# Output weights two tiles ahead, eight low parts of h on GpSimd, and the attention norm's factors inside the first weights

## The chip, the cores and the metric

One core of a Trainium2 chip. The metric is the device time of one execution in microseconds (us), and of several runs the median. Engines are named as in the profile: PE (TensorE, matrix products), ACT (ScalarE), DVE (VectorE), POOL (GpSimd), and SP, whose queue issues most of the loads and stores. Each engine executes its own instructions in the order in which they stand in the program, and waits on semaphores where it needs another's result.

## The reference

One decoder layer with model width 1024, 1024 tokens, eight sliding-window heads and eight forgetting-attention heads, and an MLP of width 4096, in float32:

```python
xn = rmsnorm(x, attn_norm_g)
proj = jnp.einsum('bsd,de->bse', xn, w_in)
...
out_a = swa_sinks_attention(qa, ka, va, sink_logits)
...
out_b = forgetting_attention(qb, kb, vb, log_f)
mixed = jnp.concatenate([out_a.reshape(b, s, A_Q_W), out_b.reshape(b, s, B_W)], axis=-1)
x = x + jnp.einsum('bse,ed->bsd', mixed, w_out)
hn = rmsnorm(x, mlp_norm_g)
hid = jnp.square(jax.nn.relu(jnp.einsum('bsd,df->bsf', hn, w_up)))
x = x + jnp.einsum('bsf,fd->bsd', hid, w_down)
```

## The kernel before

**Products.** Every operand of a product is split into a rounded high part (type fp32r) and a low part, the rest. A product is three passes: high by high, high by low, low by high. `split` (line 75) makes the two parts of one tile: a cast on one engine, and a subtraction, which reads the raw tile and the high part, on another. Both inputs of the subtraction are in SBUF.

**Start.** NWARM = 8 products on zeros come first on PE. Then the first projection runs over eight steps k of the contraction (lines 193 to 223). For each k, SP loads 128 rows of x transposed (`xr`, in two halves of 512 tokens) and 128 x 384 weights (`wr`); DVE casts the weights, POOL makes their low part (DVE for k = 0), and ACT and DVE make the two parts of x times the norm's factor `ga`. `ga` is eight columns of the small tile `vt`, which ACT's queue loads at the very start. The eight sums `qps0` to `qps7` are 128 tokens each. At k = 0 all high-by-high products come first; from k = 1 on the three passes of a token block stand together.

**Attention** fills the time up to about 437 us; other projections and the first halves of the output products (`out_first`, which leaves eight partial sums in the DRAM tensor `part_d`) are laid between its heads. The last products of output tiles 0 and 4 come at its end.

**Output stage, 437 to 477 us.** The output has eight tiles `dt` of 128 model columns by 1024 tokens. The order is 0, 4 (ahead), then 1, 5, 2, 6, 3, 7. For each, `out_weights` loads four 128 x 128 weight blocks (`wor`) and splits them into `wos` (cast on ACT, low part on POOL), `out_products` makes 24 products of 512 columns into two PSUM banks `po0`, `po1`, and `out_finish` ends the tile:

- SP loads the partial sum from `part_d` into `h`; DVE adds the two banks (line 958, one input in PSUM); SP stores `h` to `h_d`. Tiles 0 to 3 share one slot for `h`, tiles 4 to 6 another, so the next load into a slot waits for the store.
- `h` is split at once for the up products, which follow a seven-product scheme (Strassen's, in Winograd's form) over halves of the model width and of the tokens: seven operands `bh1` to `bh7` (high) and `bl1` to `bl7` (low). `bh1` comes from tiles 0 to 3, `bh2` and `bh3` from 4 to 7, and the others from sums `ts` of a tile dt and its partner dt + 4: DVE makes the sums (lines 965 and 977), ACT casts them, and DVE makes the low parts (`sum_splits`, line 985). Such a pair is one t of four.

The up weights follow from the middle of this stage: `wur` is the raw load, `wus` are four sums of its blocks made by DVE, and `wu` is a split operand (cast on ACT; low part on DVE for products 2, 6 and 5, on POOL for the others). Up products stand in the order `UP = (1, 2, 3, 6, 7, 5, 4)` and go to banks `pu1` to `pu7`, k running over t. A split operand's slot (w0 to w6) is shared with `h`, `xt` and `wos`, so a cast into it waits for what stood there.

**What sets the order.** The kernel's calls are placed by a scheduler, which has its own estimate of each instruction's length and moves instructions of an engine past each other. `tc.issue_after` keeps an instruction behind another one. From 477 us on the up products and then the down products (`pd`) run to the end, PE without a gap.

Of the kernel before, what the change touches and what calls it, by code (L numbers as in the profile page):

```python
# [16 lines left out]
P = 128  # L17
D = 1024
# [12 lines left out]
NWARM = 8  # L31
# [24 lines left out]
def hybrid_layer(  # L56
# [18 lines left out]
    def split(hi, lo, src, hi_eng, lo_eng):  # L75
        if hi_eng is nc.scalar:
            hi_eng.copy(hi, src)  # L77
        else:
            hi_eng.tensor_copy(hi, src)
        lo_eng.tensor_tensor(out=lo, in0=src, in1=hi.bitcast(F32), op=ALU.subtract)  # L80

    def rsqrt(pool, out, t, shape, tag):
# [26 lines left out]
    nc.scalar.dma_start(vt[:, :36], vecs)  # L109
    ga, gm, vec, bfb, snk = (  # L110
        vt[:, a:b] for a, b in ((0, 8), (8, 16), (16, 20), (20, 28), (28, 36))
    )
    nsnk = cp.tile([P, NH], F32, name="nsnk")
    nc.vector.tensor_scalar_mul(nsnk, snk, -1.0)
    gqk = cp.tile([P, 2], F32, name="gqk")
    for i in range(2):
        nc.vector.tensor_tensor(
            out=gqk[:, i : i + 1], in0=vec[:, 2 * i : 2 * i + 1],
            in1=vec[:, 2 * i + 1 : 2 * i + 2], op=ALU.mult,
        )  # L120

    nc.vector.tensor_scalar_mul(gqk, gqk, -0.25 / math.sqrt(HD))
# [53 lines left out]
    def w_tiles(n):  # L176


        w = wp.tile([P, 2 * WL], F32R, tag="w", name="w", bufs=8)
        wr = wp.tile([P, WN], F32, tag="wr", name="wr", bufs=3)  # L180
        lo = 384 if n == 384 else 400
        return wr[:, :n], w[:, :n], w[:, lo : lo + n]
# [10 lines left out]
    for k in range(KT):  # L193
        xr = ap2.tile([P, S], F32, tag="s", name="xr", bufs=NS)
        wr, wh, wl = w_tiles(384)
        if k == 0:
            nc.sync.dma_start(wr, w_a0[:, k, :])
            nc.scalar.preload_act_table_set("natural_log_exp_and_others")
        nc.sync.dma_start(xr[:, halves[0]], xT[k * P : (k + 1) * P, halves[0]])
        if k:  # L200
            nc.sync.dma_start(wr, w_a0[:, k, :])
        nc.sync.dma_start(xr[:, halves[1]], xT[k * P : (k + 1) * P, halves[1]])
        split(wh, wl, wr, nc.vector, nc.gpsimd if k else nc.vector)
        for cs in halves:
            hi, lo = (x_part(j, k, cs) for j in range(2))
            nc.scalar.activation(hi, xr[:, cs], AF.Copy, scale=ga[:, k : k + 1])
            last_x = nc.vector.scalar_tensor_tensor(  # L207
                out=lo, in0=xr[:, cs], scalar=ga[:, k : k + 1],
                in1=hi.bitcast(F32), op0=ALU.mult, op1=ALU.subtract,
            )  # L210
        passes = ((0, wh), (0, wl), (1, wh))
# [21 lines left out]
    def load_w(src, n):  # L233
        his, los = [], []
        for k in range(KT):
            wr, wh, wl = w_tiles(n)
            nc.sync.dma_start(wr, src[:, k, :])
            with tc.high_priority(offset=HPO):
                split(wh, wl, wr, nc.scalar, nc.gpsimd)
            his.append(wh)  # L240
            los.append(wl)
        return his, los
# [609 lines left out]
    nout = [0]  # L852

    def out_weights(dt, e0):
# [3 lines left out]
        w = slot(f"w{i % 2}", "wos", [2, 4, P], F32R)  # L858
        split(w[:, 0], w[:, 1], wr, nc.scalar, nc.gpsimd)
# [83 lines left out]
    part = {}  # L943
# [345 lines left out]
def _layout(x, attn_norm_g, w_in, b_forget, q_norm_a, k_norm_a, sink_logits,  # L1289
# [16 lines left out]
            [cols(attn_norm_g), cols(mlp_norm_g), two(q_norm_a), two(k_norm_a),  # L1306
             two(q_norm_b), two(k_norm_b), rep(b_forget), rep(sink_logits)], axis=1
        ),
        "w_a0": rows(np.concatenate([qa[:, :P], w_in[:, 512:768]], axis=1)),
# [34 lines left out]
```

## Time and profile before

| | us |
|---|---|
| runs of the kernel before | 1095.04, 1093.57, 1093.83 (median 1093.83) |
| the profiled execution | 1092.15 |
| its span, first to last instruction | 1090.4 |
| start to the first real product | 5.4 |
| projections and attention | 5.4 to 437 |
| output stage | 437 to 477 |
| up products | 477 to 782 |
| down products and the end | 782 to 1090.4 |
| ACT busy | 569.9 |
| POOL busy | 362.5 |

Times in the profile are from the span's start. A row of a timeline has the start, the length, the engine, the kernel's line, the operation and its tiles (out <- in), and how many followed without a gap (x); in brackets stands how long the engine had been idle before, and what ended that. A matmul's length is longer than its distance to the next one, because they overlap.

### The profile page before, as it was taken

Reading aid. Unit: us, or ns where it says so; the run is one execution under the profiler, and the core shown is the slowest. Engines: PE = TensorE matmul, PEld = TensorE weight load, DVE = VectorE, ACT = ScalarE, POOL = GpSimd, SP = SyncE. Lnnn points to the kernel's source line nnn. Section 1 sums busy time; section 2 is a strip of 40 time slices with the busy share of each in tenths; the row PEclk is TensorE's granted clock in tenths of the full one; section 3 lists DMA queues with packets and bytes.
Section 4 is the critical chain, followed back from the end, with each engine's and each line's share of the span. In section 5 each row is a group of like instructions: output and inputs, shape, how many; then the busy total and the mean of one; then the engine's idle time right before and its main releaser. Section 6 shows DMA issues by size and latency. Waiting matters only on the chain.

```text
span 1090.4 us, 15689 instructions
## 1 busy us (share of the span) xinstructions
PE 1078.7 (99%) x5557; PEld 933.5 (86%) x5557; DVE 777.7 (71%) x1327; ACT 569.9 (52%) x1013; POOL 362.5 (33%) x352
## 2 busy tenths in 40 slices
PE   9999999999999999999999999999999999999998
PEld 8999999999997888778888888888888888888886
DVE  7377677767765676998686869867675876674395
ACT  5558588666766756554545444353633433333331
POOL 5672523435434634333222232322222222231100
PEclk9999999999999999999999999999999999999999
DMA  9401212335656565663545543443998886665523
GB/s 308 141 27 48 72 37 61 115 87 154 209 192 221 167 223 174 212 231 126 198 179 179 189 153 135 149 170 145 333 390 311 299 289 227 241 228 181 174 87 116
DMA packets 96079, 195.69 MB, mean 179 GB/s; under 512 B 7376, under 2 KB 19584, under 8 KB 96000
## 3 DMA queue, kind: packets, MB, share of 16 engines
q1 hardware_dynamic: 95856, 194.66, 51.4%
q8 instruction: 44, 0.72, 0.3%
q14 instruction: 35, 0.29, 0.1%
q10 hardware_dynamic: 144, 0.02, 0.0%
HBM read 141.61 MB, written 53.04 MB: 179 GB/s over the span
## 4 chain that ended last, share of the span: by engine, by line
PE 82%; DMA 6%; DVE 6%; issue 2%; ACT 2%; POOL 1%; SPq 0%; ACTq 0%; POOLq 0%; DVEq 0%
PE pu L73 28%; PE pd L73 28%; PE ps L73 10%; PE po L73 5%; PE spb L73 3%; PE pvb L73 2%; PE tpb L725 2%; PE sp L73 1%; PE pv L73 1%; DMA wr<-in_w_b_dram 1%; DMA xq<-in_x_dram 1%; PE tpa L554 1%; DMA xr<-in_xT_dram 1%; DMA mixs_d<-mixn 1%; DVE x L207 1%
## 5 line engine op out<-in xcount | busy, mean ns | idle before, releaser
L73 PE MATMUL pd<-hx,wx 128*128 128x512 f32 (+1 forms) x1350 | 304.9, 388 | 0.0
L73 PEld LDWEIGHTS pd<-hx,wx 128*128 128x128 f32 x1350 | 252.7, 188 | 52.2
L73 PE MATMUL pu<-bh,wu 128*128 128x512 f32 x896 | 276.6, 390 | 1.0 <-ACT bh L947 1.0
L73 PE MATMUL ps<-w,x 128*128 128x384 f32 (+1 forms) x960 | 199.0, 345 | 0.4 <-DVE z L451 0.3
L73 PEld LDWEIGHTS pu<-bh,wu 128*128 128x128 f32 x896 | 168.1, 188 | 36.4 <-ACT bh L947 1.4
L73 PE MATMUL pu<-bl,wu 128*128 128x512 f32 x448 | 174.0, 389 | 0.0
L73 PEld LDWEIGHTS ps<-w,x 128*128 128x128 f32 x960 | 165.2, 189 | 3.7 <-DVE z L451 0.6
L77 ACT CAST hx<-hr 128x1024 fp32r<-128x1024 f32 x56 | 59.1, 1055 | 176.2 <-PE pd L73 171.2
L80 POOL TENSOR_TENSOR wx<-wda,wx 128x1024 fp32r<-128x1024 f32 x24 | 64.5, 2687 | 196.4 <-ACT wx L77 196.4
L80 DVE TENSOR_TENSOR hx<-hr,hx 128x1024 fp32r<-128x1024 f32 x56 | 72.2, 1297 | 71.0 <-ACT hx L77 71.0
L73 PEld LDWEIGHTS pu<-bl,wu 128*128 128x128 f32 x448 | 84.1, 188 | 17.7 <-issue 0.2
L73 PE MATMUL po<-mix,wos 128*128 128x512 f32 x384 | 94.8, 396 | 1.0 <-ACT wos L77 1.0
L73 PEld LDWEIGHTS po<-mix,wos 128*128 128x128 f32 x384 | 70.5, 188 | 15.5 <-ACT wos L77 1.5
L80 POOL TENSOR_TENSOR wu<-wus,wu 128x512 fp32r<-128x512 f32 x32 | 45.6, 1426 | 113.0 <-ACT wu L77 113.0
L80 POOL TENSOR_TENSOR wu<-wur,wu 128x512 fp32r<-128x512 f32 x32 | 44.2, 1380 | 102.5 <-ACT wu L77 102.5
L1018 DVE TENSOR_TENSOR ht<-hb 128x512 f32<-128x512 f32 x32 | 21.8, 723 | 62.8 <-ACT hb L1073 62.8
L394 DVE TENSOR_TENSOR ptl<-tpb,pth 128x512 fp32r<-128x512 f32 (+1 forms) x80 | 49.5, 631 | 21.9 <-ACT pth L393 18.9
L80 POOL TENSOR_TENSOR w<-wr,w 128x384 fp32r<-128x384 f32 (+1 forms) x47 | 51.5, 1106 | 40.1 <-ACT w L77 29.4
L77 ACT CAST wu<-wus 128x512 fp32r<-128x512 f32 x64 | 38.0, 618 | 48.3 <-PE pu L73 39.9
L77 ACT CAST wx<-wda 128x1024 fp32r<-128x1024 f32 x56 | 58.5, 1049 | 6.6 <-DMA wda<-in_w_d_dram 6.6
L689 ACT ACTIVATE sb<-sb,nmb 128x128 f32<-128x128 f32 (+3 forms) x64 | 49.8, 779 | 22.7 <-DVE nmb L683 22.6
L1072 ACT ACTIVATE hb<-hb 128x2048 f32<-128x2048 f32 x16 | 30.7, 1917 | 48.0 <-DVE hb L1021 47.9
(210 smaller groups left out, 1839.3 us busy)
## 6 DMA issues: line engine op xcount, KB each, us to landing
wda<-in_w_d_dram SPq DMA_DIRECT2D x34, 1024.0 KB, 9.2
hr<-hid_d SPq DMA_DIRECT2D x56, 512.0 KB, 5.7
wur<-in_w_u_dram SPq DMA_DIRECT2D x32, 512.0 KB, 4.3
hid_d<-ht SPq DMA_DIRECT2D x16, 1024.0 KB, 4.5
hid_d<-hb SPq DMA_DIRECT2D x16, 768.0 KB, 3.6
mix<-mixs_d SPq DMA_DIRECT2D x7, 1024.0 KB, 5.8
wr<-in_w_b_dram SPq DMA_DIRECT2D x32, 192.0 KB, 2.5
xr<-in_xT_dram SPq DMA_DIRECT2D x16, 256.0 KB, 5.0
```

The costliest lines, as they stand in the source:

```text
L73: return nc.tensor.matmul(out, lhsT, rhs, start=start, stop=stop)
L77: hi_eng.copy(hi, src)
L80: lo_eng.tensor_tensor(out=lo, in0=src, in1=hi.bitcast(F32), op=ALU.subtract)
L207: last_x = nc.vector.scalar_tensor_tensor(out=lo, in0=xr[:, cs], scalar=ga[:, k : k + 1], in1=hi.bitcast(F32), op0=ALU.mult, op1=ALU.subtract,
L394: nc.vector.tensor_tensor(out=lo[:, cols], in0=pt[:, cols], in1=hi[:, cols].bitcast(F32), op=ALU.subtract)
L554: nc.tensor.transpose(tp[:, hh * P : (hh + 1) * P], pts[hh // 2][:, hh % 2, c0 : c0 + P], ident)
L689: nc.scalar.activation(pr[:, :nk], pr[:, :nk], AF.Exp, scale=-1.0, bias=nm[:, c : c + 1], accum_out=dn_b[p % 2][:, h, i : i + 1] if p < 3 ...
L725: nc.tensor.transpose(tp[:, c0 : c0 + P], probs[qi][:, kb * P : (kb + 1) * P], ident)
L1018: eng.tensor_tensor(out=out, in0=a, in1=b, op=ALU.subtract)
L1072: nc.scalar.activation(b, b, AF.Relu)
```

## The change

Three things are changed.

**The start.** One warm-up product fewer. The norm's factor becomes column 384 of each 128 x 385 weight load, so no product waits for `vt`, whose load moves to a later place on ACT's queue and whose small vectors are made later. The first weights lead SP's queue. The first x tile comes in three pieces, 256, 256 and 512 tokens, the first of them by ACT's queue.

**Output weights two tiles ahead.** The weights of tiles 1 and 5 are made before tiles 0 and 4 are finished (in two more slots), and those of every later tile after the products of the tile two before it.

**Eight low parts on GpSimd.** `bl5` and `bl4` (four t each) are made by GpSimd and not by DVE, and issued after the low part of the last output weights made so far.

```diff
-NWARM = 8
+NWARM = 7
...
-        lo_eng.tensor_tensor(out=lo, in0=src, in1=hi.bitcast(F32), op=ALU.subtract)
+        return lo_eng.tensor_tensor(out=lo, in0=src, in1=hi.bitcast(F32), op=ALU.subtract)
...
-    nc.scalar.dma_start(vt[:, :36], vecs)
...
+        ga = wr[:, 384:385]
+
+        pieces = (slice(0, 256), slice(256, 512), halves[1]) if k == 0 else halves
         if k == 0:
-            nc.sync.dma_start(wr, w_a0[:, k, :])
+            nc.sync.dma_start(wr[:, :385], w_a0[:, k, :])
+        for i, cs in enumerate(pieces):
+            eng = nc.scalar if k == 0 and i == 0 else nc.sync
+            eng.dma_start(xr[:, cs], xT[k * P : (k + 1) * P, cs])
+            if k and i == 0:
+                nc.sync.dma_start(wr[:, :385], w_a0[:, k, :])
...
+        if k == 2:
+            nc.scalar.dma_start(vt[:, :28], vecs)
-        split(wh, wl, wr, nc.vector, nc.gpsimd if k else nc.vector)
-        for cs in halves:
+        split(wh, wl, wr[:, :384], nc.vector, nc.gpsimd if k else nc.vector)
+        for cs in pieces:
             hi, lo = (x_part(j, k, cs) for j in range(2))
-            nc.scalar.activation(hi, xr[:, cs], AF.Copy, scale=ga[:, k : k + 1])
+            nc.scalar.activation(hi, xr[:, cs], AF.Copy, scale=ga)
...
+        if k == 2:
+            small_vectors()
...
-        w = slot(f"w{i % 2}", "wos", [2, 4, P], F32R)
-        split(w[:, 0], w[:, 1], wr, nc.scalar, nc.gpsimd)
+        w = slot(f"w{i % 2 + (5 if i in (11, 12) else 0)}", "wos", [2, 4, P], F32R)
+        part["weights"] = split(w[:, 0], w[:, 1], wr, nc.scalar, nc.gpsimd)
...
     def sum_splits(ts, t, which):
         for i, n in which:
-            split(bh[n][:, t], bl[n][:, t], ts[:, i], nc.scalar, nc.vector)
+            last = n in (5, 4)
+            with tc.issue_after(part["weights"].ins) if last else nullcontext():
+                split(
+                    bh[n][:, t], bl[n][:, t], ts[:, i], nc.scalar,
+                    nc.gpsimd if last else nc.vector,
+                )
+    rest = (1, 5, 2, 6, 3, 7)
+    ws = [out_weights(dt, 4) for dt in rest[:2]]
...
-    for dt in (1, 5, 2, 6, 3, 7):
-        w = out_weights(dt, 4)
+    for i, dt in enumerate(rest):
         ps = [bank(f"po{c}") for c in range(2)]
-        out_products(ps, w, range(4, 8))
+        out_products(ps, ws[i], range(4, 8))
+        if i + 2 < len(rest):
+            ws.append(out_weights(rest[i + 2], 4))
         out_finish(dt, ps)
```

The scheduler places the instructions anew. In the output stage this is what stands on three engines (line, operation, out <- in, size; the number behind a tile's name tells apart tiles of one name).

On ACT, around the casts of the first up weights, before. `h_5851` is the h of tile 5, `ts_5816` the sums of the pair 1 and 5, `h_5902` the h of tile 2, `wos_5969` and `wos_6011` the output weights of tiles 3 and 7, and `wu_6063` and `wu_6082` the operands of the first two up products:

```order
L947 ACTIVATE bh3_5731<-h_5851,vt_67 128x512
L77 CAST bh6_5733<-ts_5816 128x512
L77 CAST bh7_5735<-ts_5816 128x512
L77 CAST wu_6063<-wur_5913 128x512
L77 CAST wu_6082<-wur_5913 128x512
L77 CAST bh4_5739<-ts_5816 128x512
L77 CAST wos_5969<-wor_5967 128x512
L947 ACTIVATE bh1_5727<-h_5902,vt_67 128x512
L964 ACTIVATE b12_5817<-h_5809,vt_67 128x512
L77 CAST wos_6011<-wor_6009 128x512
```

And the same place now, where tile 5's h is `h_5863`, the sums `ts_5828`, tile 2's h `h_5914`, and the weights `wos_5911` (tile 3), `wos_5956` (tile 7), `wu_6065` and `wu_6084`:

```order
L960 ACTIVATE bh3_5733<-h_5863,vt_67 128x512
L77 CAST bh6_5735<-ts_5828 128x512
L77 CAST wu_6065<-wur_5925 128x512
L77 CAST bh7_5737<-ts_5828 128x512
L77 CAST wu_6084<-wur_5925 128x512
L77 CAST bh4_5741<-ts_5828 128x512
L77 CAST wos_5911<-wor_5909 128x512
L960 ACTIVATE bh1_5729<-h_5914,vt_67 128x512
L977 ACTIVATE b12_5922<-h_5914,vt_67 128x512
L77 CAST wos_5956<-wor_5954 128x512
```

The cast of `bh7`, which read nothing but `ts` and stood ahead of both up-weight casts, now stands between them.

On DVE at the same place, before (lines 1018 and 1021 are the sums `wus`, line 958 the sum `h`):

```order
L80 TENSOR_TENSOR bl6_5734<-ts_5816,bh6_5733 128x512
L80 TENSOR_TENSOR bl7_5736<-ts_5816,bh7_5735 128x512
L958 TENSOR_TENSOR h_5902<-po0_5876,h_5902 128x512
L80 TENSOR_TENSOR wu_6082<-wur_5913,wu_6082 128x512
L958 TENSOR_TENSOR h_5902<-po1_5877,h_5902 128x512
L1021 TENSOR_TENSOR wus_6058<-wur_5913 128x512
L1018 TENSOR_TENSOR wus_6058<-wur_5913 128x512
L80 TENSOR_TENSOR bl4_5740<-ts_5816,bh4_5739 128x512
L948 SCALAR_TENSOR_TENSOR bl1_5728<-h_5902,vt_67,bh1_5727 128x512
```

And now (lines 1041 and 1044 are the sums `wus`, 971 the sum `h`):

```order
L80 TENSOR_TENSOR bl6_5736<-ts_5828,bh6_5735 128x512
L80 TENSOR_TENSOR bl7_5738<-ts_5828,bh7_5737 128x512
L1044 TENSOR_TENSOR wus_6060<-wur_5925 128x512
L1041 TENSOR_TENSOR wus_6060<-wur_5925 128x512
L80 TENSOR_TENSOR wu_6084<-wur_5925,wu_6084 128x512
L971 TENSOR_TENSOR h_5914<-po0_5883,h_5914 128x512
L971 TENSOR_TENSOR h_5914<-po1_5884,h_5914 128x512
L1041 TENSOR_TENSOR wus_6060<-wus_6060,wur_5925 128x512
L961 SCALAR_TENSOR_TENSOR bl1_5730<-h_5914,vt_67,bh1_5729 128x512
```

`bl4` has gone to POOL, and the two sums of `h` for tile 2 moved behind three operations that read the raw up weights.

On POOL, from the output weights of tiles 2 and 6 (`wos_5818`, `wos_5860`) on, where before only low parts of `wos` and `wu` stood:

```order
L80 TENSOR_TENSOR wos_5818<-wor_5816,wos_5818 128x512
L80 TENSOR_TENSOR wos_5860<-wor_5858,wos_5860 128x512
L80 TENSOR_TENSOR bl5_5740<-ts_5761,bh5_5739 128x512
L80 TENSOR_TENSOR bl4_5742<-ts_5761,bh4_5741 128x512
L80 TENSOR_TENSOR bl5_5740<-ts_5828,bh5_5739 128x512
L80 TENSOR_TENSOR wu_6065<-wur_5925,wu_6065 128x512
L80 TENSOR_TENSOR bl4_5742<-ts_5828,bh4_5741 128x512
L80 TENSOR_TENSOR wos_5911<-wor_5909,wos_5911 128x512
L80 TENSOR_TENSOR wos_5956<-wor_5954,wos_5956 128x512
L80 TENSOR_TENSOR bl5_5740<-ts_5921,bh5_5739 128x512
L80 TENSOR_TENSOR bl4_5742<-ts_5921,bh4_5741 128x512
L80 TENSOR_TENSOR wu_6105<-wus_6060,wu_6105 128x512
```

The low parts of `bl5` and `bl4` were taken in between; `bl4` of the pair 1 and 5 stands ahead of the weights of tiles 3 and 7. On PE the products of tile 1 now stand together ahead of those of tile 5 (before, four of each came first), and the first products of the first step run over token blocks 0 and 1 in the high and weight-low passes before blocks 2 and 3.

More of the change, by code (lines that the diff above doesn't have):

```diff
@@ L108, in hybrid_layer, with small_vectors @@
     vt = cp.tile([P, 68], F32, name="vt")
[L109 to L111 removed]
+    gm, vec, bfb, snk = (
+        vt[:, a:b] for a, b in ((0, 8), (8, 12), (12, 20), (20, 28))
     )
     nsnk = cp.tile([P, NH], F32, name="nsnk")
[L114 removed]
     gqk = cp.tile([P, 2], F32, name="gqk")
[L116 to L122, printed above, removed]
+    def small_vectors():
+        nc.vector.tensor_scalar_mul(nsnk, snk, -1.0)
+        for i in range(2):
+            nc.vector.tensor_tensor(
+                out=gqk[:, i : i + 1], in0=vec[:, 2 * i : 2 * i + 1],
+                in1=vec[:, 2 * i + 1 : 2 * i + 2], op=ALU.mult,
+            )
+        nc.vector.tensor_scalar_mul(gqk, gqk, -0.25 / math.sqrt(HD))
     rstd = cp.tile([P, NT], F32, name="rstd")
@@ L852, in hybrid_layer @@
     nout = [0]
+    part = {}
     def out_weights(dt, e0):
```

21 lines of the change are left out of this document (10 added, 11 removed).

## The prediction

> **What bounds the kernel now.** I read the page's busy shares first, then the busy time by stage, then TensorE's (PE's) timeline for its gaps, and last the chain of waits ahead of the last gap.
>
> ```profile
> span 1090.4 us, 15689 instructions
> PE 1078.7 (99%) x5557; PEld 933.5 (86%) x5557; DVE 777.7 (71%) x1327; ACT 569.9 (52%) x1013; POOL 362.5 (33%) x352
> ...
> 5.40:39.00 33.60, 33.60 (x193) 33.41 (x194) 20.91 (x36) 23.79 (x43) 16.98 (x14) 1.00 0.91 319
> ...
> 437.00:477.00 40.00, 38.47 (x169) 31.22 (x167) 38.31 (x55) 21.50 (x37) 9.71 (x7) 1.00 0.71 235
> 477.00:782.00 305.00, 304.88 (x1341) 251.81 (x1342) 233.15 (x313) 142.71 (x184) 92.95 (x65) 1.00 0.48 173
> ```
>
> PE is busy 1078.7 of 1090.4 us, and the change leaves the number of real products alone, so nothing but PE's gaps can be won. By stage (the columns are the length, then busy time of PE, PEld, DVE, ACT and POOL) the output stage, 437 to 477, is the odd one: DVE is busy 38.31 of its 40 us, nearly as long as PE, while POOL works only 9.71. From 477 on PE has no gap left.
>
> ```profile
> 1.28 3.32 PE L73 MATMUL qps<-warm 128*128 128x512 bf16 x8 [1.28 <-DVE warm L189]
> 5.38 5.44 PE L73 MATMUL qps<-w,x 128*128 128x384 f32 x29 [0.77 <-ACT x L206]
> ...
> 435.55 4.27 PE L73 MATMUL po<-mix,wos 128*128 128x512 f32 x18
> 440.50 21.83 PE L73 MATMUL po<-mix,wos 128*128 128x512 f32 x95 [0.69 <-ACT wos L77]
> ...
> 475.77 0.39 PE L73 MATMUL pu<-bh,wu 128*128 128x512 f32 x1
> 477.12 0.73 PE L73 MATMUL pu<-bh,wu 128*128 128x512 f32 x2 [0.97 <-ACT bh L947]
> ```
>
> Three gaps bear on the change. Real work begins at 5.38. A 512-column product is issued every (4.27 - 0.39) / 17 = 0.228 us, so the last of the 18 started at 439.43 and the step to 440.50 lost 1.07 - 0.228 = 0.84 us, waiting for ACT's cast of output weights. The step from 475.77 to 477.12 lost 1.35 - 0.228 = 1.12 us, waiting for bh1 of tile 3. The chain of waits says what stands behind that last one:
>
> ```profile
> 453.90 5.00 DMA wur<-in_w_u_dram
> 458.93 0.05 ACT wu L77
> ...
> 467.27 1.29 DVE h L958 x2
> ...
> 469.19 6.57 DMA h_d<-h
> ...
> 475.83 0.04 ACT wu L77
> ...
> 476.35 0.73 ACT bh L947
> ```
>
> It isn't PE's: it runs through DVE's h, the store of h for tile 6, and a cast on ACT whose slot that store must leave before bh1 can follow.
>
> **The start: -0.3.**
>
> ```profile
> 4.60 0.72 ACT L206 ACTIVATE x<-xr,vt 128x512 fp32r<-128x512 f32 x1 [2.08 <-DMA xr<-in_xT_dram]
> 3.84 0.36 DVE L79 CAST w<-wr 128x384 fp32r<-128x384 f32 x1 [1.31 <-DMA wr<-in_w_a_dram]
> 8.34 1.46 POOL L80 TENSOR_TENSOR w<-wr,w 128x384 fp32r<-128x384 f32 x1 [4.71 <-DVE w L79]
> ```
>
> The weights with the norm's factor are in SBUF by 3.84. The first 256 columns of x, on ACT's queue, should be there about then too; half of the 0.72 us op makes a first product near 4.6, 0.8 earlier. The first step's 24 products take 24 x 0.174 (33.60 us for 193) = 4.2 us, to 8.8, three more of the second step need no low part, and the next one does: GpSimd delivers it at 8.34 + 1.46 = 9.80. The load it hangs on keeps its fifth place on SP's queue. At 9.80 PE had done 24 + (9.80 - 9.56) / 0.174 = 25.4 products before and will have done 27: 1.6 x 0.174 = 0.3 us are won. The bounds are -0.8 (that low part earlier too) and +0.4: the small vectors' load now goes behind the table load, and DVE waits for it ahead of the low parts of x. One warm-up product fewer costs nothing if the clock rises as before: eight took 3.32 us, so seven end at about 4.2. The Trainium skill, "TensorE: Matmul & The Clock Gate", Part 1, has the full clock only after some 3.4 us of sustained work; counted from 1.28 that is 4.7, and by it the first real product would run at half rate and the gain be 0.1 to 0.2 us less. Only the first products of the changed trace can say.
>
> **The weights two tiles ahead: the 0.84 us gap goes, and 0.3 + 0.84 = 1.1 us reach the output products.** The casts of tiles 1 and 5 go to the attention's last part, where ACT is not full; I take 0 for them there (+1.2 us at most, two casts of 0.6, if a head waits for them; -0.5 if the new order suits the heads). So PE starts tile 1 at 439.1 and without waits ends tiles 1, 5, 2, 6, 3, 7 each 24 x 0.228 = 5.5 us apart: 444.6, 450.0, 455.5, 461.0, 466.4, 471.9.
>
> **The eight low parts on GpSimd: here the change turns.** POOL's rows and DVE's beside them show a lock:
>
> ```profile
> 440.53 3.07 POOL L80 TENSOR_TENSOR wos<-wor,wos 128x512 fp32r<-128x512 f32 x2 [8.82 <-ACT wos L77]
> 449.26 1.30 POOL L80 TENSOR_TENSOR wos<-wor,wos 128x512 fp32r<-128x512 f32 x1 [5.66 <-ACT wos L77]
> 464.23 1.31 POOL L80 TENSOR_TENSOR wos<-wor,wos 128x512 fp32r<-128x512 f32 x1 [1.60 <-ACT wos L77]
> ...
> 442.38 1.77 DVE L965 SCALAR_TENSOR_TENSOR ts<-h,vt,b 128x512 f32<-128x512 f32 x1
> 449.30 1.28 DVE L958 TENSOR_TENSOR h<-po,h 128x512 f32<-128x512 f32 x2
> 464.30 1.78 DVE L948 SCALAR_TENSOR_TENSOR bl<-h,vt,bh 128x512 fp32r<-128x512 f32 x1
> 466.61 0.74 DVE L965 SCALAR_TENSOR_TENSOR ts<-h,vt,b 128x512 f32<-128x512 f32 x1
> ```
>
> A DVE op on two SBUF tensors takes 0.74 us alone and 1.77 under a GpSimd low part: it waits 1.04 us until GpSimd is done. The h sums, which read PSUM, are not held (1.28 for two at 449.30). A GpSimd op that stands ready when a DVE op ends goes first. So a moved low part gives DVE 0.6 us back and takes up to 1.04, unless an h sum covers it. The Trainium skill, "SBUF — State Buffer", "Who interferes with whom", has the port go to whoever issues first: were that always DVE, with its next op already queued, the moves would be a pure gain, the second case below; the rows at 442.38 and 464.30 are against it.
>
> Tile 0/4: of bl3, ts, bl, bl, ts, bl, bl (4.56 us to the h sum at 449.30) two low parts go (1.2, and 0.1 to 0.2 that the last of them waited) and one turn of GpSimd's comes in (1.04): 0.34 less, and with the start's 0.3 the h sums of tile 1 are 0.64 us earlier.
>
> ```profile
> 450.61 0.32 SPq L959 DMA_DIRECT2D h_d<-h  x1
> ...
> 455.59 1.28 ACT L77 CAST bh<-ts 128x512 fp32r<-128x512 f32 x2
> 458.93 1.14 ACT L77 CAST wu<-wur 128x512 fp32r<-128x512 f32 x2 [2.05 <-DMA wur<-in_w_u_dram]
> ...
> 458.12 1.29 DVE L80 TENSOR_TENSOR bl<-ts,bh 128x512 fp32r<-128x512 f32 x2
> 459.33 0.69 DVE L958 TENSOR_TENSOR h<-po,h 128x512 f32<-128x512 f32 x1
> 461.39 0.68 DVE L958 TENSOR_TENSOR h<-po,h 128x512 f32<-128x512 f32 x1
> ```
>
> SP stores that h (450.61) and only then loads the next part and the up weights (wur, 453.90), so wur lands 0.64 earlier, 458.3 instead of 458.93. In the new order ACT's cast of wur stands ahead of bh7 of tile 5, so bl7, which DVE began at 458.7 before, must wait for wur; and behind bl7 DVE now has two wus sums and the low part of wu ahead of both h sums of tile 2, where before one h sum stood ahead of all of them. From wur at 458.3: GpSimd's wu low part runs 459.0 to 460.3, bl7 ends at 460.85; GpSimd's bl4 (cast by 460.5) takes its turn, 1.15; wus ends at 462.6; the low part of tile 3's output weights takes its turn to 463.75; wus, wu, then the h sums end at 465.55 and 466.15. Before, they ended at 461.39 + 0.68 = 462.07: **4.1 us later**, although DVE has fewer ops. Behind them wus, bl1, wus, one more turn of GpSimd's (tile 7's weights) and ts: h of tile 6 ends at 470.95 against 468.54, 2.4 later; its store goes at 471.0 against 469.19, 1.8 later, and with the same 6.57 us the wu cast and bh1 follow at 477.6 and 478.1 to 478.85.
>
> PE meanwhile waits about 1.9 us for tile 3's low weights (needed 461.0 + 4 x 0.228, ready 463.75), reaches the product that needs bh1 at 475.9 and waits till 478.9. Before, it went on at 477.12 with 12 up products done; the new order has 10 done: 2 x 0.228. **Shift: 478.9 - 477.12 + 0.46 = +2.2.** What was won at the start and at 439 lies inside this wait.
>
> The view of h_d gives the time of these stores:
>
> ```profile
> DMA to landing us min/median/max: 2.6/3.9/8.1
> ```
>
> From issue to landing that is 2.6 to 8.1 us. If tile 6's is quick, the DVE ops set bh1: h of tile 3 ends at 476.7, bh1 at 477.4, shift +0.75. At 8.1 it is +3.7.
>
> ```profile
> 483.90 1.78 DVE L977 SCALAR_TENSOR_TENSOR ts<-rr,vt,ts 128x512 f32<-128x512 f32 x1
> 485.60 1.77 DVE L80 TENSOR_TENSOR bl<-ts,bh 128x512 fp32r<-128x512 f32 x1
> 487.29 1.79 DVE L1021 TENSOR_TENSOR wus<-wur 128x512 f32<-128x512 f32 x1
> ```
>
> Behind bh1 (tile 7's splits, the same lock) DVE and GpSimd take turns at 1.7 us a pair; with two more GpSimd ops among them my walk has bl3 0.5 us and bl6 0.8 us behind PE. Before, the turns at 483.9 to 489 cost PE nothing. Between 0 and 1.3 I take 0.6.
>
> **Sum:** +2.2 + 0.6 = +2.8. The profiled execution took 1092.15 us, 1.75 more than its span; it would become 1094.95. It lies 1.68 below the median of the runs, 1093.83, and I set the difference on the median: 1096.6.
>
> **Rivals.** *The relief works*, 0.13: wur lands before bl6 is through, or GpSimd's ops fall beside h sums, so DVE is ahead and all three gaps close: -0.3 - 0.84 - 1.12 = -2.3, 1091.5. For it: DVE is the fullest engine behind PE and loses eight ops. Against it: two of three GpSimd ops quoted held DVE up, and the wur load follows a store. It decides at bl7: the cast of wur would have to start before 457, when bl6 ends. *Give and take*, 0.28: GpSimd's turns cost DVE what it gains, h of tile 6 ends within 1 us of 468.5, and the wait ahead of bh1 swallows what PE won: -0.3 to +0.8, 1093.5 to 1094.6. For it: the end of that wait hangs on a 6.57 us store, not on PE. *The weights come no sooner*: for tiles 3 and 7 the change does not do what it says, since their casts stand behind wur and their low parts behind DVE; that is in the forecast, and costs only if the wait behind it closes. *GpSimd late after bh1*, 0.06: the low parts of wu for products 3 and 7 queue behind bl5 and bl4, 2 us more, 1098.6.
>
> **Chances.** The forecast has 0.53, from +0.75 to +5.0 (3.7 and 1.3). I count differences beyond 0.2%, 2.19 us, as faster or slower, about what a measurement can tell from no change. Of the forecast's 0.53 some 0.40 lie above it, with the last rival 0.46 slower; 0.41 are the same; 0.13 faster. The range leaves out the relief and reaches from give and take, with 1.2 below it for the heads and the start, to the forecast's upper part: 1092.4 to 1099.0.
>
> **What would show it.** After bl6 of tile 5 DVE stands idle for wur some 2 us before bl7; h of tile 2 is written about 466 instead of 462; PE waits near 462 for a wos low part on POOL, and near 476 for bh1 longer than 1.12 us; the gap at 439 is gone; the first product stands near 4.6. If h of tile 6 comes before 468 and PE's wait for bh1 is gone, the lock or the order of the casts was read wrongly.

## The result, and the profile after

| | before | after |
|---|---|---|
| median of the runs on one chip, us | 1094.44 (6 runs, 1093.57 to 1097.29) | 1101.09 (6 runs, 1099.36 to 1103.68) |
| after over before | | 1.0056, 95% interval 1.0043 to 1.0070 |
| the profiled execution, us | 1092.15 | 1101.10 |

The change makes the kernel slower by 0.56%, some 6.1 us (4.7 to 7.7). The profile shown of the kernel before lies 2.3 us under its median here, that of the changed kernel on its own, so the two profiles differ by 9.0 and the runs by 6.1. Of 88 runs of the kernel before, timed beside the experiments, the 66 with a mean granted clock of 0.999 or more average 1093.9 us, 21 with 0.996 to 0.998 average 1096.8, and one at 0.85, left out of every comparison, took 1192.3, so that a single profile can lie 2 to 3 us off.

The page and the busy time by stage, of the changed kernel (columns as before):

```profile
span 1099.4 us, 15693 instructions
PE 1081.2 (98%) x5556; PEld 933.1 (85%) x5556; DVE 769.5 (70%) x1320; ACT 571.0 (52%) x1014; POOL 374.6 (34%) x360
```

```profile
437.00:477.00 40.00, 38.19 (x172) 30.81 (x171) 33.04 (x43) 17.55 (x31) 14.32 (x10) 1.00 0.48 163
477.00:782.00 305.00, 301.68 (x1326) 248.44 (x1325) 222.89 (x312) 144.69 (x186) 97.45 (x68) 1.00 0.47 169
```

Between 437 and 477 DVE is busy 33.04 us where it was 38.31, and POOL 14.32 instead of 9.71 (PE comes some 4 us later into this stretch now, so that it holds a little less of the stage). PE gained nothing by it. It has gaps where it had none, in the up products too (301.68 of 305, before 304.88). They are in PE's timeline:

```profile
4.71 3.57 PE L73 MATMUL qps<-w,x 128*128 128x384 f32 x19 [0.26 <-ACT x L216]
...
426.01 0.63 PE L737 MATMUL tpb<-ident,sb 128*128 128x128 f32 x4 [0.59 <-DVE dnb L708]
427.25 0.55 PE L737 MATMUL tpb<-ident,sb 128*128 128x128 f32 x3 [0.61 <-DVE ptl L406]
...
429.64 0.55 PE L737 MATMUL tpb<-ident,sb 128*128 128x128 f32 x3 [0.86 <-DVE ptl L406]
430.65 0.66 PE L737 MATMUL tpb<-ident,sb 128*128 128x128 f32 x4 [0.46 <-DVE ptl L406]
...
469.50 2.81 PE L73 MATMUL po<-mix,wos 128*128 128x512 f32 x11 [1.45 <-POOL wos L80]
...
484.11 0.50 PE L73 MATMUL pu<-bh,wu 128*128 128x512 f32 x1 [2.06 <-ACT bh L960]
...
494.76 0.73 PE L73 MATMUL pu<-bh,wu 128*128 128x512 f32 x2 [1.25 <-POOL wu L80]
```

The first real product comes at 4.71, not 5.38. The gap ahead of tile 1's products is gone. But the last attention heads have four gaps between 425 and 431 where the kernel before had one of 0.53 (transposes `tpb`, waiting for DVE), and the output stage has three: for tile 3's low weights, for bh1 (1.12 before, here 2.23 by the distance between products), and behind it for the low part of `wu`.

Following each product of PE from the one kernel to the other, I read the shift at three places and take differences: from ahead of the last heads to tile 1's first product (440.50 before) PE loses **2.04 us**, the closed gap of 0.85 already taken off; from there to the end of the stage's after-effects (500) it loses **4.59**. In the tables below these are "heads" and "output stage". The other 2.4 of the 9.0 us lie ahead of the heads. There the ten versions with the old start, whose code is that of before up to the heads, also stand 0.1 to 4.7 us behind this one profile of before (2.0 on average), so most of that is the draw of a single profile and not the change.

### The profile page after: what moved, and what is told of

It is laid out like the page before. It is cut to its first block, busy times and chain, and to the rows that moved or that the text cites. A ratio compares the mean times of both kernels' runs of the same rounds, so it can differ in the third digit from the quotient of the medians.

```text
span 1099.4 us, 15693 instructions
## 1 busy us (share of the span) xinstructions
PE 1081.2 (98%) x5556; PEld 933.1 (85%) x5556; DVE 769.5 (70%) x1320; ACT 571.0 (52%) x1014; POOL 374.6 (34%) x360
## 4 chain that ended last, share of the span: by engine, by line
PE 55%; DVE 3%; DMA 1%; issue 1%; ACT 0%; POOL 0%; SPq 0%; POOLq 0%; DVEq 0%; ACTq 0%
PE pd L73 27%; PE pu L73 27%; DVE h L971 1%; PE po L73 0%; DVE ts L990 0%; DMA wur<-in_w_u_dram 0%; DMA mix<-mixs_d 0%; DVE bl L961 0%; PE pvb L73 0%; DVE bl L80 0%; DVE ts L978 0%; DMA h_d<-h 0%; DVE wus L1041 0%; DVE m L1044 0%; DVE pd L1284 0%
## 5 line engine op out<-in xcount | busy, mean ns | idle before, releaser
L405 ACT CAST pth<-tpb 128x512 fp32r<-128x512 f32 (+1 forms) x80 | 41.8, 542 | 16.6 <-PE tpb L737 11.8
```

Of the source, the lines that this page charges most:

```text
L405: nc.scalar.copy(hi[:, cols], pt[:, cols])
```

## What holds the exponential in the heads

The ACT timeline at 422, first of the kernel before, then of the changed one:

```profile
418.24 0.83 ACT L689 ACTIVATE sb<-sb,nmb 128x640 f32<-128x640 f32 x1 [0.40 <-DVE nmb L683]
```

```profile
422.45 0.62 ACT L77 CAST wos<-wor 128x512 fp32r<-128x512 f32 x1 [2.09 <-DMA wor<-in_w_o_dram]
422.98 0.83 ACT L701 ACTIVATE sb<-sb,nmb 128x640 f32<-128x640 f32 x1
```

The maximum that this exponential needs, in DVE's timeline of the changed kernel:

```profile
420.65 0.08 DVE L695 DVE_READ_ACCUMULATOR2_ANT nmb<- 128x1 f32 x1
```

The softmax's exponential of 640 columns used to start as soon as DVE had its maximum. Now the cast of tile 5's output weights stands ahead of it and waits 2.09 us for its load, and the exponential, whose maximum is there at 420.7, starts behind it at 422.98, 2.2 us late, and with it all that follows: DVE's reciprocal (`dnb`), the low parts `ptl`, PE's transposes. The cost is not the cast's own 0.62 us but its place in a queue that is worked off in order.

## The output stage

The same pattern around the first up weights, in ACT's, DVE's and POOL's timelines of the changed kernel:

```profile
464.07 0.62 ACT L77 CAST wu<-wur 128x512 fp32r<-128x512 f32 x1 [3.63 <-DMA wur<-in_w_u_dram]
464.60 0.62 ACT L77 CAST bh<-ts 128x512 fp32r<-128x512 f32 x1
...
471.23 0.73 ACT L960 ACTIVATE bh<-h,vt 128x512 fp32r<-128x512 f32 x1 [4.45 <-DVE h L971]
```

```profile
465.25 1.37 DVE L80 TENSOR_TENSOR bl<-ts,bh 128x512 fp32r<-128x512 f32 x1 [2.21 <-ACT bh L77]
466.54 1.78 DVE L1044 TENSOR_TENSOR wus<-wur 128x512 f32<-128x512 f32 x1
468.24 1.75 DVE L1041 TENSOR_TENSOR wus<-wur 128x512 f32<-128x512 f32 x1
469.91 0.68 DVE L80 TENSOR_TENSOR wu<-wur,wu 128x512 fp32r<-128x512 f32 x1
470.52 1.28 DVE L971 TENSOR_TENSOR h<-po,h 128x512 f32<-128x512 f32 x2
```

```profile
466.34 1.44 POOL L80 TENSOR_TENSOR bl<-ts,bh 128x512 fp32r<-128x512 f32 x1 [0.27 <-ACT bh L77]
467.74 1.70 POOL L80 TENSOR_TENSOR wos<-wor,wos 128x512 fp32r<-128x512 f32 x1
```

bh7 (464.60) stands behind the cast that waits for `wur`; bl7 on DVE waits 2.21 us for bh7; two `wus` take 1.78 and 1.75 instead of 0.68, since GpSimd's bl4 and `wos` (466.34, 467.74) lie beside them; and h of tile 2, whose products were long done, ends at 471.8, 7.7 us after wur. Tile 3's low weights come off POOL at 469.4, and PE waits for them.

## The experiments

Times are ratios to the kernel before, from runs on the same chip, with 95% intervals; 0.001 is 1.1 us. "Heads" and "output stage" are PE's losses against the profile of before, as above.

| version | time over before | heads, us | output stage, us |
|---|---|---|---|
| the change | 1.0056 (1.0043 to 1.0070) | 2.04 | 4.59 |
| e1 start alone | 1.0006 (0.9993 to 1.0018) | 0.56 | 0.44 |
| e2 weights ahead alone | 1.0036 (1.0020 to 1.0052) | 1.98 | 2.28 |
| e3 low parts alone | 1.0033 (1.0022 to 1.0045) | 0.92 | 2.80 |
| e4 both, without the start | 1.0049 (1.0035 to 1.0062) | 1.99 | 4.37 |
| e5 = e2, late casts | 1.0032 (1.0018 to 1.0045) | -0.18 | 4.01 |
| e6 = change, bh7 first | 1.0075 (1.0058 to 1.0092) | 2.10 | 4.01 |
| e7 = change, both | 1.0057 (1.0040 to 1.0075) | -0.96 | 4.96 |
| e8 = change, low parts zero | 1.0050 (1.0034 to 1.0066) | 2.05 | 2.56 |
| e9 = change, wur's readers last | 1.0047 (1.0032 to 1.0062) | 2.14 | 1.96 |
| e10 = e4, late casts, wur last | 1.0032 (1.0020 to 1.0044) | 0.07 | 3.00 |
| e11 = e5, wur last | 1.0037 (1.0026 to 1.0049) | 0.07 | 2.10 |
| e12 = before, tiles 1 and 5 ahead | 1.0030 (1.0018 to 1.0042) | -0.42 | 2.35 |
| e13 = before, product 5 late | 1.0001 (0.9988 to 1.0015) | 1.12 | -0.06 |
| e14 = before, bh1 first | 1.0013 (0.9998 to 1.0027) | -0.12 | 1.22 |
| e15 = change, bh1 first | 1.0092 (1.0071 to 1.0113) | 1.76 | 7.49 |
| e16 = e10, bh1 first | 1.0016 (1.0000 to 1.0031) | -0.76 | 4.02 |

The last two columns come from one execution each, and where the code is that of before they still show 0.4 to 1.1 us (e1, e3, e13). They are read for large and repeated differences; sums are read from the times.

### The parts alone: e1 to e4

Each takes some parts of the change's diff and leaves the rest as before. e1 has only the start (the first half of the diff); e2 only the two tiles ahead:

```diff
     def sum_splits(ts, t, which):
         for i, n in which:
-            last = n in (5, 4)
...
+            split(bh[n][:, t], bl[n][:, t], ts[:, i], nc.scalar, nc.vector)
```

e3 has only the low parts on GpSimd, e4 everything but the start:

```diff
-    ws = [out_weights(dt, 4) for dt in rest[:2]]
-    for i, dt in enumerate(rest):
+    for dt in rest:
+        w = out_weights(dt, 4)
...
-        out_products(ps, ws[i], range(4, 8))
+        out_products(ps, w, range(4, 8))
```

> The start's part alone: the norm's factor in the first weights, one warm-up product fewer, the new order of loads; weights of the output stage and low parts as before. Theory (tie): a split of x now waits for the weight tile that carries the factor, and there are three such tiles, so the x loads, the squares of x behind them and rstd come later. The first product stands 0.6 to 0.7 us earlier, yet PE is about 1.5 us late after the wait near 68 us, and the run is 1.3 to 2.5 us slower than before. Rival (carried): what is won at the first product stays: 0.3 to 0.7 us faster. Rival (absorbed): the waits at 67 and 77 take it: within 0.3 us.

> The output weights two tiles ahead alone; start and low parts as before. Theory (heads): the casts of the weights of tiles 1 and 5, now between the last heads' casts and exponentials on ACT, and their low parts on GpSimd, hold the last heads up: PE is 2 to 3 us late between 420 and 437, the gap of 0.84 us at 439 goes, and the chain to bh1, which starts from the attention's end, is late too: 1.5 to 3 us slower. Rival (covered): ACT has room there, the gap at 439 goes and is lost again or not: 0.8 us faster to no change.

> The eight low parts on GpSimd alone; start and weights as before. The cast of bh7 of tile 5 stands ahead of the up weights' casts here, as before the change. Theory (lock): DVE operations on two SBUF tensors wait for each moved low part, so DVE gains little: h of tile 6 within 1 us of 468.5, bh1 within 1.5 us of 477; behind bh1 GpSimd is late for up products: in sum 0 to 2 us slower. Rival (relief): DVE is ahead by 0.6 us for each moved part, h of tile 6 is ended by 466, the wait of 1.1 us for bh1 goes: about 1 us faster.

> The changed kernel with its start undone: weights ahead and low parts on GpSimd, start as before. bh7 of tile 5 stands behind the first up-weight cast, as in the changed kernel. Theory (parts add): the start's loss of 1.5 to 2.5 us goes and the rest stays: 4 to 5.5 us slower than before instead of 6.6. Rival (swallowed): the waits of the output stage set the end whatever the start does: as slow as the changed kernel, 6 to 7 us. Second rival: the start is the whole loss: within 1 us of before.

The start alone changes nothing that the runs can tell, as the rival called absorbed had it; the loss of 1.3 to 2.5 us expected of it did not come. The weights ahead cost 3.9 us alone and the low parts 3.6, each beyond the range expected of it, and together 5.4: both are losses, neither undoes the other. The 5.4 of e4 lie in the range expected, but not because a loss of the start went. e2's heads show the held exponential without the low parts (its cast waits 2.02 us for the load), and e2's gap at 439 is gone. e3's wait for bh1 is gone, but PE waits 2.29 us for POOL's low part of tile 3's weights. Of these four only e4, which has both parts, has bh7 behind wur's cast, as the change has.

### The two orders: e5, e6, e7

e5 holds the casts of tiles 1 and 5's weights on ACT until the last head's last cast, with their loads where the kernel before had them, tile 1's as early as in e2, tile 5's some 3.6 us later. e6 puts bh7 of tile 5 ahead of wur's casts. e7 has both.

```diff
+        with tc.issue_after(mark) if mark else nullcontext():
+            part["weights"] = split(w[:, 0], w[:, 1], wr, nc.scalar, nc.gpsimd)
...
+    ws = [out_weights(dt, 4, head_cast[0]) for dt in rest[:2]]
...
+            with tc.issue_after(part[7, 1]) if j == 0 and n in (1, 2) else nullcontext():
+                split(w[:, 0], w[:, 1], src[n], nc.scalar, nc.vector if n in (2, 6, 5) else nc.gpsimd)
```

> The weights two ahead alone, but the casts of tiles 1 and 5's weights are held on ACT until the last attention head's last cast of mix; their loads still go early. Theory (a cast that waits for its load at the head of ACT's queue holds the exponential behind it): the 2.5 us lost in the heads between 422 and 436 go, the gap at 439 stays gone; about 2.5 us faster than the weights two ahead alone (1100.24), that is 1097 to 1098, and 0.5 to 3 above the kernel before. Rival (the load traffic or the casts themselves cost the heads): the loss in the heads stays, time as the weights two ahead alone, within 1 us.

> The changed kernel, with bh7 of tile 5 cast ahead of the casts that wait for wur; nothing else moves on ACT. Theory: DVE's idle time of 2.2 us before bl7 goes, the sums wus begin when wur lands and h of tile 2 follows wur by some 5.5 us instead of 7.2; PE's wait for tile 3's low weights (1.62) falls by 1 or more and the wait for bh1 (2.23) to between 0.8 and 1.5; the time falls by 1 to 1.7 us against the changed kernel. Rival (DVE waits for wur in any case, behind bl7 stand only operations that read it): no change beyond 0.5 us; h of tile 2 stays at wur + 6.5 or more.

> The changed kernel with both corrections: tiles 1 and 5's casts after the heads, and bh7 ahead of wur's casts. If the two causes are separate and add: 2.5 + 1 to 1.7 us faster than the changed kernel (1101.1), that is 1097 to 1097.6. If the wait for bh1 sets the time whatever comes before it: no more than e6 alone gains. If the held exponential was all: as much as e5 gains against the weights two ahead alone.

In the heads the traces agree with the theory. In e5 the exponential starts 0.40 us after DVE's maximum again and the casts come when ACT is free:

```profile
420.50 0.83 ACT L691 ACTIVATE sb<-sb,nmb 128x640 f32<-128x640 f32 x1 [0.40 <-DVE nmb L685]
...
440.02 1.15 ACT L79 CAST wos<-wor 128x512 fp32r<-128x512 f32 x2
```

All seven profiles with the early casts (the change, e2, e4, e6, e8, e9, e15) lose 1.76 to 2.14 us there, all six with late casts (e5, e7, e10, e11, e12, e16) -0.96 to 0.07. Holding the casts moves loads too (tile 5's stands at 422.41 in e5, at 418.91 in the changed kernel), so e5 doesn't separate the cast from load traffic; that it is the cast rests on the rows above, where the maximum was there, ACT idle, and the exponential 2.2 us late. In the times, though, e5 stands where e2 stood (0.4 us apart, with some 2.3 either way; by the medians alone 1100.24 in e2 and 1097.22 in e5, 5.5 and 3.5 us above the kernel before): its output stage loses 4.01 us instead of 2.28, and what the heads had won was given back there. That was not expected, and by the times alone e5 doesn't confirm the theory.

The traces show where it was given back. These are ACT's first casts of `wur`, first in e2 and then in e5:

```profile
461.30 1.15 ACT L77 CAST wu<-wur 128x512 fp32r<-128x512 f32 x2 [1.76 <-DMA wur<-in_w_u_dram]
...
462.87 1.14 ACT L79 CAST wu<-wur 128x512 fp32r<-128x512 f32 x2 [2.71 <-DMA wur<-in_w_u_dram]
```

PE starts tile 1 0.2 us earlier in e5, but wur is cast 1.57 later, and this makes up the 1.73 between 2.28 and 4.01. SP loads wur behind the next part of h, which waits till the store of tile 1's h has landed. In e5 that store is issued 0.62 later (453.58, 452.96), since the low parts of four output weights now lie beside DVE's work between 440 and 451 where two did, and it lands 3.78 us on instead of 2.93.

e6 is a miss. In DVE's timeline the idle time only moved from ahead of bl7 to behind it:

```profile
466.83 0.69 DVE L1047 TENSOR_TENSOR wus<-wur 128x512 f32<-128x512 f32 x1 [2.31 <-DMA wur<-in_w_u_dram]
...
470.81 1.28 DVE L973 TENSOR_TENSOR h<-po,h 128x512 f32<-128x512 f32 x2
```

What stands behind bl7 reads wur itself, as the rival had it. h of tile 2 ends 7.2 us after wur (464.89 in ACT's row there) instead of 7.7; the wait for bh1 fell to 1.61, that for tile 3's weights stayed (1.74). e7 is a miss as well: its heads lose nothing any more, its output stage 4.96, and its time is that of the change.

### The port: e8

The low parts bl5 and bl4 are set to zero by GpSimd early on (their values are left out); ACT and DVE keep their order.

```diff
+                if last:
+                    nc.scalar.copy(bh[n][:, t], ts[:, i])
+                    nc.gpsimd.memset(bl[n][:, t].bitcast(F32), 0.0)
```

> The changed kernel with the eight low parts bl5 and bl4 not made but set to zero by GpSimd, which reads no SBUF tensor for that and does it early (left out: the low parts of two of seven up operands). ACT and DVE keep their order. Theory (GpSimd's turns on the shared port hold DVE): two to three turns of about 1.1 us go from DVE's chain between 445 and 477, h of tile 2 comes about 1 us sooner after wur (6 instead of 7.2), and behind bh1 the wait of 1.41 us goes: 1.5 to 3 us faster than the changed kernel. Rival (the order of the casts alone does it, the port costs nothing): h of tile 2 stays at wur + 7, and the time within 0.7 us of the changed kernel.

```profile
463.86 1.37 DVE L80 TENSOR_TENSOR bl<-ts,bh 128x512 fp32r<-128x512 f32 x1 [2.63 <-ACT bh L77]
465.15 0.68 DVE L1045 TENSOR_TENSOR wus<-wur 128x512 f32<-128x512 f32 x1
465.75 1.77 DVE L1042 TENSOR_TENSOR wus<-wur 128x512 f32<-128x512 f32 x1
467.45 0.68 DVE L80 TENSOR_TENSOR wu<-wur,wu 128x512 fp32r<-128x512 f32 x1
468.05 1.28 DVE L971 TENSOR_TENSOR h<-po,h 128x512 f32<-128x512 f32 x2
```

With bl4 gone from POOL the first `wus` takes 0.68 us instead of 1.78, and h of tile 2 starts 4.2 us after bl7 instead of 5.3: one turn of GpSimd's costs DVE 1.1 us, close to the 1.04 of the rows of before. The waits for tile 3's weights and behind bh1 are gone, that for bh1 stays (2.06), and DVE's idle time ahead of bl7 too (2.63). The output stage loses 2.56 instead of 4.59. The 1.5 to 3 us expected in the times are not shown: they don't separate e8 from the change.

### What reads wur, last: e9 to e12

On DVE behind the two h sums of tile 2, on ACT behind bh7, bh4 and tile 3's weights:

```diff
+        with tc.issue_after(part["h", 2]) if j == 0 else nullcontext():
+            plus(s[:, 0], a21, a22)
...
+            with tc.issue_after(part["cast", 3]) if first else nullcontext(), (
+                tc.issue_after(part["h", 2]) if first else nullcontext()
+            ):
+                split(w[:, 0], w[:, 1], src[n], nc.scalar, nc.vector if n in (2, 6, 5) else nc.gpsimd)
```

e9 is this in the changed kernel, e10 in e4 with the late casts, e11 in e5. e12 is the kernel before with tiles 1 and 5 ahead only, late casts, and h of tile 2 first.

> The changed kernel with everything that reads the first wur held back: on DVE behind the two h sums of tile 2, on ACT behind bh7, bh4 and the cast of tile 3's weights. Theory (the order around wur makes the loss of the output stage): DVE's wait for wur falls beside work that comes first anyway, h of tile 2 ends before wur lands or within 1 us of it (7.7 after it in the changed kernel), PE's wait for tile 3's low weights (1.62) goes, the wait for bh1 (2.23) falls to 1 or less; 2 to 3.5 us faster than the changed kernel, 3 to 4 above the kernel before. Rival (GpSimd's turns set DVE's pace whatever the order): h of tile 6 moves by less than 1 us, the waits stay, time within 1 us of the changed kernel.

> Weights two ahead and low parts on GpSimd with the start of before, the casts of tiles 1 and 5's weights after the heads, and the order around wur as in e9. If heads (2.0) and output stage (2 to 3.5) are the whole loss and add: within 1.5 us of the kernel before, with the gap at 439 gone. Rival (GpSimd's turns and the wait behind bh1 remain): 3 to 4 above it.

> As e10, but the low parts stay on DVE: weights two ahead, late casts, the order around wur. Of e5's 4.0 us lost in the output stage the wait for tile 3's weights (0.58 + 0.48) and the excess of the wait for bh1 (0.4) should go; the wait for bl behind bh1 (1.2) has nothing to do with wur and stays: 1.5 to 2 us faster than e5, 1 to 2 above the kernel before. If order alone sets it: equal to the kernel before or up to 0.8 faster.

> The kernel before with only tiles 1 and 5's weights loaded ahead (casts after the heads) and h of tile 2 ahead of what reads wur; the later weights as before, low parts on DVE, old start. If DVE's chain follows PE through the output stage: the gap of 0.84 us at 439 is won to the end, 0.5 to 1 us faster than the kernel before. If the wait ahead of bh1 swallows it, as the prediction has it: gap gone, wait for bh1 grown by 0.8, no change.

In e9's DVE timeline the h sums of tile 2 stand right behind bl7 and end before wur lands:

```profile
464.55 1.28 DVE L82 TENSOR_TENSOR bl<-ts,bh 128x512 fp32r<-128x512 f32 x2
465.75 1.28 DVE L974 TENSOR_TENSOR h<-po,h 128x512 f32<-128x512 f32 x2
468.18 0.69 DVE L1048 TENSOR_TENSOR wus<-wur 128x512 f32<-128x512 f32 x1 [1.15 <-DMA wur<-in_w_u_dram]
```

The wait for tile 3's weights is gone, that for bh1 is 1.43, and the output stage loses 1.96 instead of 4.59. The times (1.0047 against 1.0056) agree with less than that and don't exclude it. The wait behind bh1 stays (1.46). e10 and e11 miss: PE, now earlier, waits longer for bh1 (2.44 and 2.28 instead of 1 or less). e12 shows where the closed gap goes: its wait for bh1 is 0.77, less than before, but two waits for output weights (0.62, 0.48) and one for bl behind bh1 (0.85) are new, and the time is 1.0030, a loss of 3.3 us. Closing the gap at 439 won nothing in this order.

### What holds bh1: e13 to e16

In both kernels the cast for up product 5, whose slot the store of tile 6's h must leave, stands ahead of bh1 on ACT. e13 issues that split behind bh1, in the kernel before; e14 those of products 6 and 5 behind bh1 and bl1; e15 is e14's move in the changed kernel, e16 in e10.

```diff
+            with tc.issue_after(part["h_split", 1, 3]) if (j, n) == (0, 5) else nullcontext():
+                split(w[:, 0], w[:, 1], src[n], nc.scalar, nc.vector if n in (2, 6, 5) else nc.gpsimd)
```

> The kernel before with one move: the split of the first weights of up product 5, whose cast waits at the head of ACT's queue for the store of tile 6's h, is issued behind bh1 of tile 3. Theory (bh1 is held by the order, not by data): h of tile 3's left half is written by 473.7, so bh1 comes by 474.5, before PE arrives at 475.77; bl1 on DVE is next late, by 0.3 to 0.7; the wait of 1.12 falls to 0.3 to 0.7 and the time by 0.4 to 0.8 us. Rival (the store or DVE's chain holds PE anyway): the wait stays at 1 or more, no change.

> The kernel before with the splits of products 6 and 5 both behind bh1 and bl1 of tile 3, on ACT and DVE. Theory: wait at 476 below 0.4, 0.7 to 1.1 us faster than the kernel before, if no wait for bl6 of tile 7 (it now stands behind two sums wus) takes its place. Rival: a wait of 1 us or more for bl6 appears near 485 and the time is unchanged or longer.

> The changed kernel with the same move as e14. In it h of tile 3's left half is written at 482.3 and PE arrives at 481.65, so bh1 can come at 483.0 and not 484.06: the wait of 2.23 falls to 1.0 to 1.5, the time by 0.7 to 1.2 us; the wait of 1.4 behind it stays. If the store held PE by itself: no change.

> Weights two ahead and low parts on GpSimd with the start of before, and every order mended: casts of tiles 1 and 5's weights after the heads, what reads the first wur behind h of tile 2, products 6 and 5's splits behind bh1. Theory (all of the loss but GpSimd's turns is order): the wait for bh1 (2.44 in e10) falls to 1 or less, the wait of 1.46 behind it stays: 1.3 to 1.8 us faster than e10, 1.5 to 2.5 above the kernel before. If the two moved parts were a gain once the order is right: at or below the kernel before.

ACT's timeline of e13, and behind it PE's:

```profile
475.51 0.73 ACT L947 ACTIVATE bh<-h,vt 128x512 fp32r<-128x512 f32 x1
477.43 0.62 ACT L77 CAST wu<-wus 128x512 fp32r<-128x512 f32 x1 [1.20 <-DMA h_d<-h]
...
485.17 0.62 ACT L77 CAST wu<-wus 128x512 fp32r<-128x512 f32 x1 [1.72 <-DMA h_d<-h]
```

```profile
485.84 0.50 PE L73 MATMUL pu<-bh,wu 128*128 128x512 f32 x1 [0.86 <-ACT wu L77]
```

bh1 comes ahead of the store's landing and PE's wait for it is gone, so that wait was one of order. But 8 us on PE waits 1.02 us for the next cast whose slot the next store must leave, and the time is the same. e14 likewise (1.19 for a `wu`, 1.00 for a bl). e15 is a miss in sign: the wait for bh1 fell to 1.31 as expected, but the low parts of tile 7 came later and PE waits 2.10 for one of them: 1.0092, worse than the change. In e16 DVE's last low parts lie beside GpSimd's:

```profile
483.09 1.79 DVE L985 SCALAR_TENSOR_TENSOR ts<-rr,vt,ts 128x512 f32<-128x512 f32 x1
484.80 3.45 DVE L82 TENSOR_TENSOR bl<-ts,bh 128x512 fp32r<-128x512 f32 x2
```

```profile
484.36 3.33 POOL L82 TENSOR_TENSOR wu<-wur,wu 128x512 fp32r<-128x512 f32 x2
```

Three DVE ops of about 0.7 us take 5.2, and PE waits 2.08 for the second bl, more than the 1.46 expected there; the wait for bh1 is 0.62. The time came out as expected: e16 has every part of e4 and only other orders, and stands at 1.0016 (1.0000 to 1.0031) where e4 stands at 1.0049 (1.0035 to 1.0062). About 3.6 of e4's 5.4 us (an estimate from the two intervals: 1.4 to 5.9) were order. By the profiles the heads give 2.75 of it and the output stage 0.35. With e15, which order alone made slower than the change, it is what the times show of order. What is left in e16 is hardly told from nothing, and no version was faster than the kernel before.

## Why the prediction was right and wrong

The direction was the forecast one, the size was not: some 6.1 us on the median against +2.8, and 1101.1 lies beyond the range's 1099.0.

**The weights two tiles ahead: the failed step.** The prediction costed the two casts in the heads at 0, with +1.2 at most "if a head waits for them", two casts of 0.6. A head did wait, but for the cast's load: the cast stands at the head of ACT's queue, waits 2.09 us there, and the exponential waits behind it. With the gap of 0.85 at 439 gone, as forecast, the part came out at +2.04 and not -0.84, much alike in seven profiles, and went in all six where these casts were held till after the heads. The prediction went by ACT's fill there and not by what each cast waits for, although the order of the instructions was known. By the profiles that is 2.9 us, most of the miss. The times bear it out only in part: e5 against e2 and e7 against the change show no gain, because wur came later (e5) or for a cause not found (e7); e16 against e4 shows 3.6 us, of which the profiles put 2.75 into the heads.

**The start, -0.3.** The first product came 0.67 earlier (4.71, near the forecast 4.6), but alone the start shows no gain in the times, and a term of 0.3 is below what these runs can tell. In PE's rows the gain is gone before 70 us: between 39 and 68 us the seven kernels with the new start lose 0.3 to 3.2 us (1.5 on average) and the ten with the old one -0.6 to 0.9 (0.1). In the changed kernel PE waits there for POOL's low weights (0.37 us) and twice for `z`, which DVE makes with the norm's factors `rstd` (0.48, and 0.82 where 0.28 was). The prediction has no such wait.

**The output stage, +3.9 (the +2.8 and the 1.1 that were to reach it): right in its steps up to bh1, and a little more, 4.59.** DVE idles 2.21 for bl7 (2 forecast); h of tile 2 ends 7.7 us after wur (7.85 forecast); PE waits 1.62 for tile 3's low weights (1.9), and 2.23 for bh1 (3.0), where 1.12 was before. The wait behind it is 1.41; "between 0 and 1.3 I take 0.6". The forecast start of tile 1, 439.1, is a slip: 440.50 less 0.84 and 0.3 is 439.4, which takes 0.3 off the wait forecast for tile 3's weights and leaves the sum as it is. e8 shows that the first and the last of these PE waits need GpSimd's turns, e9 that the first needs the order around wur as well, e13, in the kernel before, that the store holds bh1 only because a cast stands ahead of it.

**What was won at the start and at 439 does not reach the end**, as the prediction said, but not always inside the wait for bh1: in e12, which closes the gap, that wait shrinks to 0.77 and three other waits take its place.

**The rivals.** Relief is refuted as it was to be: its condition, wur's cast ahead of bl6's end, is not met (464.07, when bl6 had ended 1.0 us before). Give and take is refuted too: h of tile 6 ends at 476.6 and not within 1 us of 468.5, and even less the 4.4 us that PE comes later it is 3.6 late. That the weights of tile 3 come no sooner was so, in PE's wait of 1.62. The lock is what the rows of before showed, and e8's. GpSimd late after bh1 came true in part: PE's last wait is for POOL's `wu`, 1.41 and not 2 us, beside the forecast and not in its place.

**Open:** whether the runs of e9 gained the 2.6 us that its profile shows, and why those of e7 show nothing of the 2.6 that its heads and output stage together gained.

## What to carry to other kernels

Work that is moved earlier brings its waits along: at its new place on an in-order engine, look up what it waits for and which urgent instruction stands behind it, not only whether the engine has room. A load may go early while the cast that waits for it goes late; check what the late cast then stands beside. And where the engine behind PE is nearly full, a gap closed or an order mended can just move the wait on (e12, e13) or make it longer (e15).

## What the hardware showed beside this

**A wait of 2 us can cost 1.1 to 1.6 us more behind it.** e8 waits 2.06 us for bh1 until 481.60; a little later its products run at half rate (the last columns are PE's granted clock, the DMA share and GB/s):

```profile
479.00:482.50 3.50, 1.60 (x7) 1.00 (x6) 3.07 (x6) 2.19 (x4) 0.00 (x0) 0.96 1.03 418
482.50:485.50 3.00, 3.00 (x8) 2.30 (x7) 2.96 (x5) 2.59 (x5) 1.39 (x1) 0.50 1.01 404
485.50:488.00 2.50, 2.50 (x12) 2.07 (x11) 2.50 (x5) 2.43 (x6) 1.10 (x1) 0.97 0.51 202
```

Of the output stages' nine waits over 2 us (in the change, e3, e4, e7, e8, e10, e11, e15, e16) five were followed by such a stretch of some 3 us (e3, e4, e8, e15, e16), 1.1 to 1.6 us lost each, counted from products 0.427 us apart instead of 0.228; none of those of 1.75 or less was, unless a longer one stood beside it. Elsewhere shorter waits did it in pairs: near 338 us two of 0.8 to 1.5 us, 1.4 to 1.7 us apart, were followed by half rate in six profiles (e1, e4, e6, e9, e11, e15) and not in two (e7, e8). The Trainium skill, "TensorE: Matmul & The Clock Gate", Part 1, names an idle window of about 3.4 us for this; here 2.06 was enough. It also has the full clock only after some 3.4 us of work: the changed kernel's first real products, 3.4 us after the first warm-up, ran at full rate in its profile (19 in 3.57 us), which agrees; in e5, with the old start, the first products up to 10.5 us, some 15, ran at half rate (0.32 us apart, later 0.174), though in the profile of before those of the same start ran at full rate.
